# A two-layer gated-DeltaNet backbone on one core: one masked product stored at once, context units placed in another phase, masks of four heads in one instruction

## The chip, the core and the metric

The kernel runs on one NeuronCore of a Trainium2 chip. The metric is the device time of one execution in microseconds (us). One engine multiplies matrices (PE), one works on vectors (DVE), one evaluates functions (ACT), one is general (POOL); nearly all transfers are started from the queue of SP. The engines run side by side and wait for each other through semaphores. All of PE's instructions stand in an order that the program writes out itself; the order on the other engines is made by a scheduler from priorities.

## What is computed

```
for layer in 2 layers:                     # 2048 latent tokens, 256 context tokens, width 1024
    h = rms_norm(x) * (1 + scale) + shift
    xa, bg, cg, za, q, k, v, zb, b, a = split(h @ w_in)       # 4096 columns and 16
    q, k, v = silu(conv3(q, k, v)); q, k normalised           # 4 heads of 128
    o = deltanet(q, k, v, b, a, forwards) + deltanet(..., backwards)
    y = concat(bg * conv3(cg * xa) * silu(za), rms_norm(o) * silu(zb))
    x += gate * (y @ w_out)                # context tokens: in the first layer alone
out = rms_norm(x)
```

The latent scans of a direction start from the state that the context scan of that direction ended in. All products are float32 quality: a projection is three products of split operands.

## The kernel before

**Chunks and tasks.** The 18 groups of 128 tokens are five chunks: 0 is the context (2 groups), 1 to 4 are the latents (4 groups each). `project` (L326) is one task: 24 products that give 128 columns of the projection for one chunk. Columns come in units: 12 of q, k and v (`qkv`, three for each head), 16 of the convolution mixer (`mix`), 4 of the gate `zb`. `phase` (L584) runs a list of tasks; each unit's weights are loaded, split by ACT (L312) and subtracted by POOL (L314), or half by DVE and half by POOL where `shared` is set, which is so when the phase has one chunk alone. `edge` (L1066) runs units over one chunk and then backwards over the next; `pairs` runs each unit over all chunks before the next unit. A layer is: a short context phase, phase 1 (chunks 1 and 2), phase 2 (chunks 3 and 4), and `output` (L958), with 48 products for each token group.

**The written order.** Between the products of a task `pump` (L177) lets other jobs issue PE work. A job is a generator that yields how many us of PE work, by the planner's clock `Order.now`, are to pass before it goes on, or a condition. `until` (L188) moves that clock on when a condition is not met yet: then the jobs' work stands in the order with no projection between it.

**Preparation (`delta`, L619).** A job J handles 16 items (a head and a group): two heads over 8 groups. J00 and J01 belong to phase 1 of the first layer, J02 and J03 to its phase 2, J10 to J13 to the second layer; J0c and J1c are the context's. Each item loads its record (L637) into one of three buffers and two rows (L639), transposes and multiplies on PE (L658, L660), masks two products by `dm` in one DVE instruction into U (L669) and stores k and v (L675); `ITEM` = 3.8 us are yielded between items. At item 8 a job waits until the job before it is done (L648), because three U tiles of 8 KB are all there are. Then comes the tail: coefficients (L679 to L697), the inversion of 32x32 blocks by 31 steps of two DVE instructions (L728, L730), transfers that reorder blocks (L710 to L735), a yield of 50 + 2n us (82 for 16 items, L751), the merging products on PE (from L754 on; the first of them is called z1 here), and the store of U to the record in DRAM (L804).

**Scans (`scan`, L808).** A scan goes over groups: it loads a record tile `rc` of 1.5 MB (one of two buffers), masks two parts of it for each head on POOL (L832), and runs five products for each of four heads. The scans take turns with the token loads by a lock named "rc". F0a and F0b are the forward latent scans of the first layer (8 groups each), F0c the backward one (16), C00 and C01 the context's; F1a to F1c are those of the second layer. F0b waits for F0a and J03. A group's output waits for F0c's result of it.

**Order around the change.** In the first layer the 20 context tasks of `mix` and `zb` stand in phase 2 (L1122). They read context activations that are loaded again (`reload`, L384) into two of the U buffers, so that job ("again", L1117) waits for J03. In the second layer no such tasks exist. J jobs start when unit `qkv[5]` or `qkv[11]` is done and the gates of both chunks are there (L1079 to L1083, L1101, L1111).

Of the kernel before, what the change touches and what calls it, by code (L numbers as in the profile page):

```python
# [32 lines left out]
RECB = 3  # L33
HOP = 2.2
# [3 lines left out]
ITEM = 3.8  # L38
# [3 lines left out]
class Pool:  # L42
# [5 lines left out]
    def tile(self, shape, dtype, tag=None, bufs=None, name=None):  # L48
# [9 lines left out]
        assert size == own, (tag, size, own)  # L58
# [4 lines left out]
def hybrid_backbone_kernel(ctx_stack: ExitStack, tc: tile.TileContext,  # L63
# [369 lines left out]
    def chunks_in(L, ps, loaded=()):  # L433
# [5 lines left out]
        z = {}  # L439
        for n, (p, i) in enumerate(halves):  # L440
# [10 lines left out]
            if i + 2 == m:  # L451
                done.add(("h", L.l, p))
                if p in (0, 1, 3):
                    z = {"z": small_tile("g_z" if p else "g_z0"), "g": g0, "n": 0}
                yield from logits(L, p, z["z"][:, z["n"]:z["n"] + m, :])
                z["n"] += m
                if p in (0, 2, 4):
                    spawn(("g", L.l, p), gates(L, z["g"], z["n"], z["z"][:, 0:z["n"], :]))
# [72 lines left out]
    def qkv_unit(L, s, h):  # L531
# [4 lines left out]
        def consume(ci, a):  # L536
# [6 lines left out]
            nc.sync.dma_start(out=L.rec_d[g0:g0 + n, :, h, 128 * (3 - s):128 * (4 - s)].rearrange("g p t -> p g t"), in_=y.rearrange("p (g t) -> p g t", t=128))  # L543
# [40 lines left out]
    def phase(L, units, tasks, after={}, ready={}):  # L584

        w = dict(ready)
        seen = []
        left = {}
        for j, p in tasks:
# [29 lines left out]
    def delta(L, items, with_out, before):  # L619
# [26 lines left out]
        yield 7.0  # L646
        for i, (h, g) in enumerate(items):
            if i == 8 and before is not None:  # L648
                yield lambda: before in done
            if i % 8 == 0:  # L650
                U.append(dp.tile([128, 8, 2, 128], F32, tag="u", bufs=3, name="U"))
# [3 lines left out]
            with urgent():  # L655
                tp = pt()
                for s in range(s0, 3):
# [11 lines left out]
                nc.vector.tensor_tensor(U[i // 8][:, i % 8, 0:w_, :], kp[:, 0:128 * w_].rearrange("p (s t) -> p s t", t=128),  # L669
                                        dm.unsqueeze(1).to_broadcast([128, w_, 128]), ALU.mult)  # L670
# [524 lines left out]
```

## Time and profile before

| | us |
|---|---|
| median of 3 runs (3021.18 to 3025.34) | 3023.2 |
| the profiled execution | 3020.82 |
| its span, first to last instruction | 3019.1 |
| PE busy in it | 2652.3 (88%) |
| mean granted clock of PE | 0.947 of full speed |

The page gives each engine's busy time, the waits say whom an engine waited for, the chain says what ended last at each moment, and the windows give the busy time of each engine in a stretch. A busy PE is not PE at its peak: records of products overlap, so PE's rate is read from start to start.

### The profile page before, as it was taken

The numbers are of one execution on the slowest core, as the hardware profiler recorded it, in microseconds if no ns is written. First come the engines' busy times: TensorE is split into PE (matmuls) and PEld (weight loads), VectorE is DVE, ScalarE is ACT, GpSimd is POOL, SyncE is SP. The second block draws the span as 40 slices with busy tenths as digits, with TensorE's granted clock in tenths as the row PEclk, the third lists the DMA queues.
The fourth block names the chain that finished last, engine by engine and source line by source line (L and its number), as shares of the span: only waits on it lengthen the run. The fifth ranks groups of instructions, "written<-read, shape, count | busy, mean of one in ns | idle before, by whom it ended". The sixth has DMA issues, their size and how long they took to land. (4 is left out here: it accounts for less than half of the span.)

```text
span 3019.1 us, 48183 instructions
## 1 busy us (share of the span) xinstructions
PE 2652.3 (88%) x17431; PEld 2214.9 (73%) x17431; DVE 1652.2 (55%) x3972; ACT 1165.4 (39%) x3072; POOL 1012.4 (34%) x1045
## 2 busy tenths in 40 slices
PE   5898899899999489769998899998999999677898
PEld 3776778668878379768777677776788777566787
DVE  3676655555573444544133676655556746345665
ACT  2535433433544322443013544333535432423442
POOL 1332333322233113454344423332322323114543
PEclk9899999999999789889999899999999999889999
DMA  6545734356554365675755556434566533566754
GB/s 205 162 132 168 223 91 139 104 191 193 172 145 120 82 202 187 237 259 189 235 160 162 166 135 187 129 101 100 180 191 179 147 113 90 182 244 204 251 179 117
DMA packets 573323, 502.18 MB, mean 166 GB/s; under 512 B 100010, under 2 KB 528540, under 8 KB 564380
## 3 DMA queue, kind: packets, MB, share of 16 engines
q1 hardware_dynamic: 573084, 499.10, 55.1%
q8 instruction: 138, 2.26, 0.3%
q14 instruction: 101, 0.83, 0.1%
HBM read 369.86 MB, written 129.14 MB: 165 GB/s over the span
## 5 line engine op out<-in xcount | busy, mean ns | idle before, releaser
L153 PE MATMUL d<-h,whi 128*128 128x512 f32 x2048 | 861.3, 421 | 20.6 <-ACT whi L312 15.5
L153 PE MATMUL d<-h,wlo 128*128 128x512 f32 x2048 | 815.7, 398 | 41.2 <-POOL wlo L314 41.2
L153 PE MATMUL d<-l,whi 128*128 128x512 f32 x2048 | 809.8, 395 | 0.0
L314 POOL TENSOR_TENSOR wlo<-raw,whi 128x1024 fp32r<-128x1024 f32 (+1 forms) x178 | 417.0, 2343 | 564.0 <-ACT whi L312 539.8
L153 PEld LDWEIGHTS d<-h,wlo 128*128 128x128 f32 x2048 | 392.1, 191 | 135.1 <-POOL wlo L314 49.2
L153 PEld LDWEIGHTS d<-h,whi 128*128 128x128 f32 x2048 | 393.4, 192 | 104.0 <-ACT whi L312 18.3
L153 PEld LDWEIGHTS d<-l,whi 128*128 128x128 f32 x2048 | 393.6, 192 | 73.5
L153 PE MATMUL d<-who,yy 128*128 128x512 f32 x1088 | 362.8, 401 | 19.4 <-ACT yy L991 18.8
L312 ACT CAST whi<-raw 128x1024 fp32r<-128x1024 f32 x178 | 186.3, 1047 | 192.4 <-PE d L153 127.2
L153 PEld LDWEIGHTS d<-who,yy 128*128 128x128 f32 x1088 | 206.0, 189 | 66.8 <-ACT yy L991 19.0
L832 POOL TENSOR_SCALAR_AFFINE_SELECT rc<-rc 128x256 f32<-128x256 f32 (+1 forms) x288 | 111.0, 422 | 307.8 <-DMA rc<-rec_d 266.6
L153 PE MATMUL d<-wlo,yy 128*128 128x512 f32 x544 | 213.4, 392 | 0.0
L668 POOL TENSOR_TENSOR nk<-nk,phalf 128x1 f32<-128x1 f32 x144 | 85.6, 594 | 362.6 <-DVE nk L667 328.9
L728 DVE TENSOR_TENSOR tmp<-Lt,X 64x31 f32<-64x31 f32 (+15 forms) x310 | 134.8, 435 | 60.7 <-DMA Lt<-blk 48.8
L730 DVE TENSOR_TENSOR X<-X,tmp 64x31 f32<-64x31 f32 (+15 forms) x310 | 127.8, 412 | 7.2
L992 POOL TENSOR_TENSOR yy<-ys,yy 128x512 fp32r<-128x512 f32 x68 | 94.1, 1395 | 102.5 <-ACT yy L991 96.2
L340 DVE SCALAR_TENSOR_TENSOR y<-d,par,y 128x504 f32<-128x504 f32 (+2 forms) x116 | 80.0, 689 | 87.3 <-ACT y L337 87.0
L153 PE MATMUL d<-hc,whi 128*128 128x256 f32 x320 | 100.7, 315 | 28.6 <-ACT whi L312 23.8
L541 ACT ACTIVATE d<-y 128x512 f32<-128x512 f32 (+1 forms) x116 | 65.5, 565 | 143.4 <-DVE y L341 129.1
L153 PEld LDWEIGHTS d<-wlo,yy 128*128 128x128 f32 x544 | 103.2, 190 | 18.6
L884 DVE SCALAR_TENSOR_TENSOR r<-c,eg,rc 128x128 f32<-128x128 f32 x272 | 76.7, 343 | 69.4 <-PE c L153 68.6
L896 DVE TENSOR_SCALAR wk<-c,cs 128x128 f32<-128x128 f32 x288 | 80.8, 342 | 61.8 <-PE c L153 61.6
(397 smaller groups left out, 4605.2 us busy)
## 6 DMA issues: line engine op xcount, KB each, us to landing
rc<-rec_d SPq DMA_DIRECT2D x68, 1536.0 KB, 7.1
raw<-in_w_in_dram SPq DMA_DIRECT2D x178, 512.0 KB, 4.8
rec<-rec_d SPq DMA_DIRECT2D x136, 192.0 KB, 2.5
wm<-in_w_mod_dram SPq DMA_DIRECT2D x24, 1024.0 KB, 8.2
rec_d<-y SPq DMA_DIRECT2D x96, 256.0 KB, 3.0
rows<-row_d SPq DMA_DIRECT2D x144, 128.0 KB, 3.7
rec_d<-rec SPq DMA_DIRECT2D x144, 128.0 KB, 2.5
ys<-y_d SPq DMA_DIRECT2D x68, 256.0 KB, 3.8
```

The source lines that it names most:

```text
L153: nc.tensor.matmul(o, a, b, start=start, stop=stop)
L312: nc.scalar.copy(hi, raw)
L314: eng.tensor_sub(lo[:, k], raw[:, k], hi[:, k].bitcast(F32))
L340: nc.vector.scalar_tensor_tensor(d3[:, :, 1:segs], s3[:, :, 0:segs - 1], w[0], d3[:, :, 1:segs], ALU.mult, ALU.add)
L541: nc.scalar.activation(a, y, AF.Tanh, scale=0.5)
L668: nc.gpsimd.tensor_tensor(nk[:, i:i + 1], nk[:, i:i + 1], phalf[:, 0:1], ALU.pow)
L728: nc.vector.tensor_tensor(t3, L3[:, j + 1:32, j:j + 1].to_broadcast([2 * nb, m_, k]), X3[:, j:j + 1, 0:k].to_broadcast([2 * nb, m_, k]), A ...
L730: nc.vector.tensor_sub(X3[:, j + 1:32, 0:k], X3[:, j + 1:32, 0:k], t3)
L832: nc.gpsimd.affine_select(out=m, in_=m, pattern=[[0, w_], [1 - 2 * d, 128]], compare_op=ALU.is_ge, fill=0.0, base=0, channel_multiplier=2 ...
L884: nc.vector.scalar_tensor_tensor(r[:, h, :], at(p1, h), e_(L.eg, h), vn[h], ALU.mult, ALU.subtract)
L896: nc.vector.tensor_scalar(wk[:, h, :], at(p2, h), cs(2 + d, h), None, ALU.mult)
L992: nc.gpsimd.tensor_sub(l_, yr, h_.bitcast(F32))
```

## The change

The record of an item is laid out anew (k, v, second product P, kT, qT, first product V). P, the masked second product, goes from the item straight into the record and is stored with k and v; U holds V alone, at half the size, in the same ring of 24 KB. A job's wait for the job before moves from item 8 to the end of the items. An item's load becomes two DMAs. `ITEM` is 2.8; J jobs start at `qkv[0]` and `qkv[8]` and wait for their second chunk's gates and second head inside. Gates are computed for each chunk (five times a layer, before three). For J02, J03, J12 and J13 (`fast`) the tail has high priority and yields 60. The 20 context tasks stand in phase 1, on activations loaded again into the two `rc` buffers, under the "rc" lock, after C01; the tokens of chunks 3 and 4 are loaded once they are done. Weights are halved between DVE and POOL for every unit that is not followed by another task of its own. A scan masks all heads in one instruction (V first, then P) and yields 0.7 ahead of its fifth product.

```diff
-ITEM = 3.8
+ITEM = 2.8
...
-            h = L.hs[0] = h_tiles(0)
+            h = L.hs[0] = [dp.tile([128, 3, D], F32R, tag="rc", bufs=2, name=t).rearrange("p a b -> p (a b)")[:, 0:256 * KT].rearrange("p (k t) -> p k t", t=256)
+                           for t in ("hc", "lc")]
...
+                z = small_tile("g_z")[:, 0:m, :]
+                yield from logits(L, p, z)
+                spawn(("g", L.l, p), gates(L, g0, m, z))
...
+        single = {j: tasks[t + 1:t + 2] == [] or tasks[t + 1][0] != j for t, (j, p) in list(enumerate(tasks))[::-1]}
-                w[j] = weights(w_in[L.l], units[j][0], len(set(p for _, p in tasks)) == 1)
+                w[j] = weights(w_in[L.l], units[j][0], single[j])
...
-                nc.sync.dma_start(out=rec[:, 1:4 - s0].rearrange("p s t -> p (s t)"), in_=L.rec_d[g, :, h, 128:512 - 128 * s0])
+                nc.sync.dma_start(out=rec[:, 1, :], in_=L.rec_d[g, :, h, 128:256])
+                nc.sync.dma_start(out=rec[:, 2:4 - s0].rearrange("p s t -> p (s t)"), in_=L.rec_d[g, :, h, 384:640 - 128 * s0])
...
-        yield 7.0
+        yield 9.0
         for i, (h, g) in enumerate(items):
-            if i == 8 and before is not None:
-                yield lambda: before in done
             if i % 8 == 0:
-                U.append(dp.tile([128, 8, 2, 128], F32, tag="u", bufs=3, name="U"))
+                U.append(dp.tile([128, 8, 128], F32, tag="u", bufs=3, name="U"))
+            if i + 2 in wants:
+                yield lambda: done.issuperset(wants[i + 2])
...
-                nc.vector.tensor_tensor(U[i // 8][:, i % 8, 0:w_, :], kp[:, 0:128 * w_].rearrange("p (s t) -> p s t", t=128),
-                                        dm.unsqueeze(1).to_broadcast([128, w_, 128]), ALU.mult)
+                nc.vector.tensor_mul(U[i // 8][:, i % 8, :], kp[:, 0:128], dm)
...
-                nc.sync.dma_start(out=L.rec_d[g, :, h, 0:256], in_=rec[:, 0:2].rearrange("p s t -> p (s t)"))
+                if with_out:
+                    nc.vector.tensor_mul(rec[:, 2, :], kp[:, 128:256], dm)
+                nc.sync.dma_start(out=L.rec_d[g, :, h, 0:256 + 128 * (w_ - 1)], in_=rec[:, 0:1 + w_].rearrange("p s t -> p (s t)"))
             yield ITEM
         held.discard("items")
+        if before is not None:
+            yield lambda: before in done
+        first = tc.high_priority(offset=HP) if fast else nullcontext()
+        first.__enter__()
...
-        yield 50.0 + 2.0 * n
+        first.__exit__(None, None, None)
+        yield 60.0 if fast else 50.0 + 2.0 * n
...
-                for h in hd:
-                    m = rc[:, h, 4:4 + w_, :]
-                    nc.gpsimd.affine_select(out=m, in_=m, pattern=[[0, w_], [1 - 2 * d, 128]], compare_op=ALU.is_ge, fill=0.0, base=0, channel_multiplier=2 * d - 1)
+                for z in (5, 2) if with_out else (5,):
+                    m = rc[:, :, z, :]
+                    nc.gpsimd.affine_select(out=m, in_=m, pattern=[[0, NH], [1 - 2 * d, 128]], compare_op=ALU.is_ge, fill=0.0, base=0, channel_multiplier=2 * d - 1)
...
+            yield 0.7 if with_out else HOP
+            with urgent():
                 if with_out:
                     pw = pscan("c1")
...
-            yield HOP - (0.9 if with_out else 0.0)
+            yield 0.6 if with_out else 0.0
...
-        jobs = {("unit", qkv[5]): J(0), ("unit", qkv[11]): J(1), ("unit", mix[3][1]): load_second}
+        jobs = {("unit", qkv[0]): J(0), ("unit", qkv[5]): flag("qkv", l, 0, 1), ("unit", qkv[8]): J(1), ("unit", qkv[11]): flag("qkv", l, 0, 3)}
+        tasks = edge(qkv[:5], 1, 2) + pairs(qkv[5:] + mix[0], (1, 2))
+        if L.ctx_out:
...
+            behind((f"C{l}1",), "again", again, "rc")()
+            behind((f"J{l}1",), "mods", lambda: mod_job(l, L.P, 8, 12))()
+            tasks += pairs(sum(mix[1:], []), (1, 2, 0)) + pairs(mix[0] + zb, (0,))
+            jobs["chunk", 0] = lambda: (done.add(("ctx", l)), load_second())
...
-            behind((f"J{l}3",), "again", again)()
-            tasks += pairs(zb, (3, 4)) + pairs(mix[2] + mix[3], (3, 4, 0)) + pairs(zb + mix[0] + mix[1], (0,))
-        else:
-            tasks += pairs(mix[2] + mix[3], (3, 4)) + edge(zb, 3, 4)
-        phase(L, units, tasks, jobs)
+        phase(L, units, edge(qkv[:5], 3, 4) + pairs(qkv[5:] + sum(mix, []), (3, 4)) + edge(zb, 3, 4), jobs)
```

## Rows read from the trace of the kernel before

**Rows 1.** The page's first part: busy time, share of the span and instructions of each engine.

```profile
PE 2652.3 (88%) x17431; PEld 2214.9 (73%) x17431; DVE 1652.2 (55%) x3972; ACT 1165.4 (39%) x3072; POOL 1012.4 (34%) x1045
```

**Rows 2.** The windows view, cut where the program's stages change: phase 1 of the first layer; phase 2 up to its first context task; the gap there; the last stretch of context tasks; the first output stage; phase 2 of the second layer; its output stage up to the end of F1c, in two pieces. Columns: stretch and length, busy us (and instructions) of PE, its weight loads, DVE, ACT, POOL, then the granted clock, the DMA share and GB/s.

```profile
130.00:623.20 493.20, 449.02 (x3025) 364.32 (x3023) 310.22 (x721) 212.74 (x553) 159.55 (x152) 0.97 0.50 140
623.20:1005.70 382.50, 364.25 (x2313) 301.44 (x2314) 211.80 (x535) 167.07 (x449) 117.36 (x122) 0.98 0.56 166
1005.70:1098.90 93.20, 37.40 (x569) 32.85 (x568) 41.95 (x106) 15.01 (x28) 8.11 (x15) 0.65 0.46 133
...
1243.90:1356.00 112.10, 70.27 (x554) 68.22 (x552) 51.38 (x124) 48.89 (x146) 57.81 (x58) 0.84 0.77 254
1356.00:1616.00 260.00, 252.75 (x1373) 203.21 (x1373) 81.68 (x206) 48.88 (x140) 107.81 (x96) 0.99 0.61 185
...
2152.00:2613.00 461.00, 439.83 (x2889) 365.68 (x2889) 259.22 (x626) 191.03 (x481) 144.73 (x138) 0.97 0.53 153
2613.00:2742.00 129.00, 79.27 (x599) 71.55 (x598) 60.68 (x170) 37.21 (x118) 25.31 (x55) 0.81 0.65 227
2742.00:2912.00 170.00, 151.49 (x913) 131.96 (x914) 106.80 (x262) 74.69 (x273) 84.41 (x102) 0.96 0.69 228
```

**Rows 3.** The waits of PE over the whole span: engine, tile and line that waited, for whom; us in total, times, longest us.

```profile
PE d L153 <- POOL wlo L314: 42.8, 17, 6.4
...
PE t L153 <- DMA tf<-blk: 37.3, 1, 37.3
```

**Rows 4.** The same view for 2613 to 2742 us alone.

```profile
PE c L153 <- DMA rc<-rec_d: 21.9, 4, 17.6
```

**Rows 5.** The timeline of J03's tail (start us, length us, engine, line, operation): the first coefficient on DVE and the first merging product z1 on PE with the wait ahead of it.

```profile
993.72 0.16 DVE L679 TENSOR_SCALAR rk<-ssk 128x16 f32<-128x16 f32 x1
...
1048.60 0.32 PE L153 MATMUL t<-tf,U 32*32 32x32 f32 x4 [37.27 <-DMA tf<-blk]
```

**Rows 6.** The chain of work that ended last, in order of time (start us, length us, what, how many): products of a scan, the first coefficient of J13, its z1, its last store, and the outputs at the end.

```profile
2235.33 1.79 PE c L153 x16
...
2501.68 1.12 DVE rk L679
...
2602.95 1.86 PE t L153 x128
...
2631.23 8.02 DMA rec_d<-U
...
2917.00 88.46 PE d L153 x390
```

**Rows 7.** The windows view of line 669 alone, one instruction for each item: J12's 16 items, and the first 8 of J13. Columns: stretch and length, DVE busy us (and items), clock, DMA share, GB/s.

```profile
2268.00:2352.00 84.00, 6.64 (x16) 1.00 0.61 180
2360.00:2405.00 45.00, 3.32 (x8) 1.00 0.59 144
```

**Rows 8.** The windows view of line 730 alone; the bounds are the first L728 and the end of the last L730 of the inversions of J03, J12 and J13.

```profile
1018.40:1041.80 23.40, 10.63 (x31) 0.50 0.00 0
2373.60:2409.40 35.80, 12.55 (x31) 1.00 0.49 138
2523.40:2556.50 33.10, 12.39 (x29) 1.00 0.18 48
```

**Rows 9.** The windows view of line 896 alone, four instructions for each scan tile: the context's scans C00 and C01, the last five tiles of F0c, F1a, and F1c.

```profile
300.00:362.00 62.00, 4.45 (x16) 0.94 0.79 234
...
1335.00:1415.00 80.00, 5.62 (x20) 0.87 0.63 208
2200.00:2291.00 91.00, 8.98 (x32) 0.96 0.68 212
...
2711.00:2912.00 201.00, 17.99 (x64) 0.93 0.66 219
```

**Rows 10.** POOL's groups by shape (busy us and mean ns behind the bar): the masks of a scan for one head, two products and one.

```profile
L832 POOL TENSOR_SCALAR_AFFINE_SELECT rc<-rc 128x256 f32<-128x256 f32 x272 | 106.7, 429 | 290.2 <-DMA rc<-rec_d 256.3 <-PE c L153 11.6 <-PE d L153 9.0
...
L832 POOL TENSOR_SCALAR_AFFINE_SELECT rc<-rc 128x128 f32<-128x128 f32 x16 | 4.2, 302 | 17.6 <-DMA rc<-rec_d 10.3 <-PE c L153 7.3
```

**Rows 11.** The timeline inside J12's inversion: POOL subtracts weights, and one inversion step on DVE.

```profile
2382.97 2.43 POOL L314 TENSOR_TENSOR wlo<-raw,whi 128x1024 fp32r<-128x1024 f32 x1 [2.11 <-ACT whi L312]
...
2383.17 2.47 DVE L730 TENSOR_TENSOR X<-X,tmp 128x220 f32<-128x220 f32 x1
```

**Rows 12.** The waits of SP's queue over the whole span, and below it those of 2300 to 2350 us: the item loads.

```profile
SPq L637 <- DMA rec_d<-rec: 287.0, 121, 7.5
...
SPq L637 <- DMA rec_d<-rec: 21.7, 10, 3.8
```

**Rows 13.** The waits of PE from 130 to 623 us: two that belong to items.

```profile
PE t L160 <- DMA rec<-rec_d: 6.1, 2, 4.0
...
PE t L160 <- ACT rec L674: 3.5, 2, 3.1
```

**Rows 14.** The timeline of two products of a context task, one after the other.

```profile
1639.75 0.28 PE L153 MATMUL d<-lc,whi 128*128 128x256 f32 x1
1639.87 0.28 PE L153 MATMUL d<-hc,wlo 128*128 128x256 f32 x1
```

**Rows 15.** The windows view of a stretch in which items, an inversion and the convolutions of q, k and v meet (columns as in rows 2), and the masked product of an item by its durations (line 669, ns min/median/max; the shape 128x128 is that of the second layer's context).

```profile
850.00:900.00 50.00, 46.34 (x209) 37.77 (x209) 41.66 (x111) 20.59 (x71) 14.54 (x14) 0.97 0.52 138
...
L669 DVE TENSOR_TENSOR U<-o,dm x111: 269/415/425, 140.9 to 2502.7; 128x256 f32<-128x256 f32 x103, 128x128 f32<-128x128 f32 x8
```

More of the change, by code (lines that the diff above doesn't have):

```diff
@@ L33 @@
 RECB = 3
+REC = (512, 384, 128)
 HOP = 2.2
@@ L57, in tile @@
         ring, own = self.rings[tag]
-        assert size == own, (tag, size, own)
+        assert size == own or tag == "u", (tag, size, own)
         return ring.tile(shape, dtype, name=name)
@@ L438, in chunks_in @@
             xs.append(tokens_in(L, *halves[len(xs)]))
-        z = {}
         for n, (p, i) in enumerate(halves):
@@ L617, in phase, with delta @@
             pump()
-    def delta(L, items, with_out, before):
+    def delta(L, items, with_out, before, wants={}, fast=False):
         n = len(items)
@@ L871, in scan @@
                 yield t + RECORD - Order.now
-            kn, vn, kT, qT, V_, P_ = ([rc[:, h, s, :] for h in hd] for s in range(6))
+            kn, vn, P_, kT, qT, V_ = ([rc[:, h, s, :] for h in hd] for s in range(6))
             cs = lambda k, h: L.cs[:, g, k, h:h + 1]
@@ L1081, in J @@
             items = [(h, g) for h in hs for g in gs]
-            return behind((("g", l, 4 if i > 1 else 2),) + wants, f"J{l}{i}",
-                          lambda: delta(L, items, True, f"J{l}{i - 1}" if i else f"J{l}c"))
+            p = 3 if i > 1 else 1
+            return behind((("g", l, p),) + wants, f"J{l}{i}",
+                          lambda: delta(L, items, True, f"J{l}{i - 1}" if i else f"J{l}c", wants={4: (("g", l, p + 1),), 8: (("qkv", l, i // 2, hs[1]),)}, fast=i > 1))
         until(("h", l, 0))
@@ L1097, in layer, with again @@
         free = {("chunk", 1): flag("free", l, 3), ("chunk", 2): flag("free", l, 4)}
-        more = {}
-        if l == 0:
-            more[qkv[11]] = behind(("J01",), "mods", lambda: mod_job(l, L.P, 8, 12))
-        jobs = {("unit", qkv[5]): J(0), ("unit", qkv[11]): J(1), ("unit", mix[3][1]): load_second}
-        if l == 0:
-            jobs["unit", mix[0][0]] = more[qkv[11]]
-        phase(L, units, edge(qkv[:5], 1, 2) + pairs(qkv[5:] + sum(mix, []), (1, 2)) + edge(zb, 1, 2), {**jobs, **free})
+        jobs = {("unit", qkv[0]): J(0), ("unit", qkv[5]): flag("qkv", l, 0, 1), ("unit", qkv[8]): J(1), ("unit", qkv[11]): flag("qkv", l, 0, 3)}
+        tasks = edge(qkv[:5], 1, 2) + pairs(qkv[5:] + mix[0], (1, 2))
+        if L.ctx_out:
+            done.discard(("h", l, 0))
+            def again():
+                reload(L)
+                done.add(("h", l, 0))
+                yield lambda: ("ctx", l) in done
+            behind((f"C{l}1",), "again", again, "rc")()
+            behind((f"J{l}1",), "mods", lambda: mod_job(l, L.P, 8, 12))()
+            tasks += pairs(sum(mix[1:], []), (1, 2, 0)) + pairs(mix[0] + zb, (0,))
+            jobs["chunk", 0] = lambda: (done.add(("ctx", l)), load_second())
+        else:
+            tasks += pairs(sum(mix[1:], []), (1, 2))
+            jobs["unit", mix[3][1]] = load_second
+        phase(L, units, tasks + edge(zb, 1, 2), {**jobs, **free})
         lat = list(range(2, NG))
@@ L1110, in layer @@
         wo = {}
-        jobs = {("unit", qkv[5]): J(2, *(("mods",) if l == 0 else ())), ("unit", qkv[11]): J(3),
+        jobs = {("unit", qkv[0]): J(2, *(("mods",) if l == 0 else ())), ("unit", qkv[5]): flag("qkv", l, 1, 1),
+                ("unit", qkv[8]): J(3), ("unit", qkv[11]): flag("qkv", l, 1, 3),
                 ("chunk", 3): lambda: out_weights(L, 0, wo), ("chunk", 4): lambda: out_weights(L, 4, wo)}
-        tasks = edge(qkv[:5], 3, 4) + pairs(qkv[5:] + mix[0] + mix[1], (3, 4))
-        if L.ctx_out:
-            done.discard(("h", l, 0))
-            def again():
-                reload(L)
-                done.add(("h", l, 0))
-                yield 0.0
-            behind((f"J{l}3",), "again", again)()
-            tasks += pairs(zb, (3, 4)) + pairs(mix[2] + mix[3], (3, 4, 0)) + pairs(zb + mix[0] + mix[1], (0,))
-        else:
-            tasks += pairs(mix[2] + mix[3], (3, 4)) + edge(zb, 3, 4)
-        phase(L, units, tasks, jobs)
+        phase(L, units, edge(qkv[:5], 3, 4) + pairs(qkv[5:] + sum(mix, []), (3, 4)) + edge(zb, 3, 4), jobs)
         at_tile = {}
```

37 lines of the change are left out of this document (15 added, 22 removed).

## The prediction

> **What bounds the kernel now.** I read the page's engine line first: PE is busy 88% of the span [rows 1], so PE's work is the floor and its idle time the stock that a change of order can take from. The windows by stage say where that stock lies: length less PE busy is 44 us in phase 1 of the first layer, 18 us in the start of its phase 2, 56 us in the gap, 42 us in the last context stretch, 7 us in its outputs; in the second layer 21 us in phase 2, then 50 and 19 us in the outputs [rows 2]. The clock falls with the idle time: 0.65 of full speed in the gap, 0.84 in the context stretch, 0.81 after phase 2 of the second layer, 0.97 or more where PE runs on [rows 2]; products there run partly at 1.2 instead of 2.4 GHz. Then the waits: one single wait of 37.3 us for the reordered inverse of J03 [rows 3, 5], and 21.9 us for scan records behind J13 [rows 4]. Both say the same: at the end of each phase 2 the preparation J03 or J13 is late, and nothing else stands in PE's order. In the first layer the projections that could fill the gap read context activations that wait for J03's buffers; in the second no projections are left.
>
> **Prices on PE.** A latent product starts every 88.46 / 390 = 0.227 us [rows 6], so a task is 24 x 0.227 = 5.45 us and an output group 48 x 0.227 = 10.9 us. A scan product starts every 1.79 / 16 = 0.112 us [rows 6]; five products, four heads, two instructions each give 40 x 0.112 = 4.5 us for a scan tile. A context product takes 0.12 us [rows 14], a context task 24 x 0.12 = 2.9 us.
>
> **When J12 and J13 end after the change.** J12 starts at the tenth task instead of the twelfth: 2 x 5.45 us, and about 1.6 scan tiles of 4.5 us between them (F1a runs there, a tile in 91 / 8 = 11.4 us [rows 9]), 18 us; the first yield is 2 longer, so its items start 16 us earlier than some 2270 [rows 7], about 2254. Items come every 84 / 16 = 5 us or a little less now [rows 7], which is ITEM, the item's own PE work and the step of the planner; with ITEM 1.0 less I take 4.0 us, 64 us for 16: to 2318. J13's items no longer wait at the eighth for J12: 2318 + 10 + 64 = 2392. The tail asks for z1 63 us after the first coefficient (60 and a step of the planner). What the other engines need is 54.9 us in J03, where POOL was idle (993.72 to 1048.60 [rows 5]); in J13 the inversion was 33.1 instead of 23.4 us [rows 8], which gives 65 us. So z1 comes about on time, 2318 + 63 = 2381. From z1 to the last store J13 took 2631.2 - 2603.0 = 28 us [rows 6]: J12 is done at 2409, after J13's items. J13's tail then runs 2409 + 63 + 28 + 2 = 2502, against 2631: **129 us earlier**.
>
> **Second layer.** F1b starts at 2502 instead of 2640 and takes 8 x 11.4 = 91 us plus the 11 us that the planner holds a record: done at 2604, inside phase 2. Phase 2 ended at 2152 + 461 + 5 = 2618 [rows 2]; F1b's PE work adds 8 x 4.5 = 36 us, and some 5 tiles of F1c that fit ahead of its end another 22: 2676. The outputs then need 16 x 10.9 = 174 us, the 11 tiles left of F1c 50 us, other PE work 14 us (of the 277 us from 2742 to the end, 166 are outputs that are left, 58 are 13 tiles of F1c, 18.5 idle and 7 low clock [rows 2], 14 the drain after the last product [rows 6]), the drain 14 us, and half the idle time, 9 us: 2676 + 261 = 2937. **Gain 82 us.** F1c is not the bound: at 201 / 16 = 12.6 us a tile [rows 9] it ends near 2810, and outputs would last to 2937 anyway.
>
> **First layer.** Phase 1 takes 12 context tasks in threes at 2.9 us and 8 alone, where weights for each task must be made: 12 tasks of that kind took 112 us with scans between them [rows 2]; I take 3.9 us with the halved subtraction, bounds 2.9 and 9.3. Sum 35 + 31 = 66 us: phase 1 ends at 623 + 66 = 689. Phase 2 becomes the second layer's: 382 us for the first 50 tasks [rows 2], 14 x 5.45 = 76, F0b 36, J03's merging products some 10 (128 took 1.86 us [rows 6], with waits between): 504. By the second layer's distances F0b ends 2604 - 2152 = 452 us after the phase begins, and 4 tiles of F0c fit behind it, 18 us: 689 + 522 = 1211. The outputs took 260 us [rows 2] with F0c's last 5 tiles [rows 9]; 12 instead of 5 add 32: 1503, against 1616. **Gain 113 us**: the gap, the context stretch and their clock.
>
> **Costs.** The two halves of a masked product cost DVE 2 x 0.27 instead of 0.415 us [rows 15], 0.13 us on each of 136 items, 17 us of DVE beside PE; four more calls of gates are some 4 us of DVE each (an estimate: 24 small operations of 0.16 us as in [rows 5]). Where DVE is fullest it has 41.7 of 50 us [rows 15]; three more items in 50 us at 1.2 us and the split's 1.5 us make 47: no bound yet, but PE waits grow. I charge 0.15 us to each of 128 latent items, 19 us, bounds 0 and 0.4 (phase 1 has 9.6 us of such waits in its 40 items, 0.24 each [rows 13]). For the four fast tails z1 may come before its data: bounds 0 and 12 us each, taken 5, 20 us with the clock; 12 because J12's inversion took 35.8 us. The new `zb` edge in the first layer has waits like those for `wlo` [rows 3], 10 us taken, bounds 0 and 15. An item's further DMA is one more issue on SP; the scan's new yield only moves 0.7 of 1.3 us: nothing, hidden by the 11 us hold; bounds -5 and 5. Masks: 302 ns for 128 and 429 for 256 columns [rows 10] make 683 for 512, so two instead of four take 1.37 instead of 1.72 us, V for all heads after 0.68; POOL is idle for its record when it starts [rows 10], so at most 0.35 us for each of 32 backward tiles, 0 to 11 us, taken 0. The reload waits for C01 and can hold PE at the 35th task if it is late; C01 was over at 362 [rows 9], and 34 tasks of 493 / 64 = 7.7 us [rows 2] put that task at 130 + 262 = 392, so 0, bounds 0 and 30.
>
> Sum: 82 + 113 - 19 - 20 - 10 = 146, and against that the earlier edges with halved weights, 0 to 10, taken 5: **151 us**. 3020.8 - 151 = 2870 for the profiled execution (its span and 1.7 us around it); the median is 2.4 us above it: **2872**.
>
> **A rule against a term.** In J12 one inversion step, 0.34 us on average with POOL idle (10.63 / 31 [rows 8]), took 2.47 us while POOL subtracted weights for 2.43 us [rows 11]; with POOL idle the 31 steps took 23.4 us, beside it 35.8 [rows 8]. The Trainium skill, page "SBUF — State Buffer", section "Who interferes with whom", says that a DVE instruction with two SBUF inputs and a GpSimd instruction that reads SBUF exclude each other for a whole instruction; the trace agrees. By that rule high priority cannot shorten the tail to its free length, and the halved weight subtraction saves less than half.
>
> **Rivals.** (1) *POOL holds the inversion.* As told ahead of the rule, as a mechanism here: each fast tail meets five or six weight subtractions and, where a scan runs, longer masks; inversions of 36 to 40 us make the tail 68 to 72 us, 5 to 9 beyond what the order allows, and each stall starts a stretch at 1.2 GHz, some 4 us. Four tails: 36 to 52 us instead of 20, so 2888 to 2904. For it: two of three inversions are that long [rows 8]. Against: at a yield of 82 z1 waited once alone, where nothing else stood in the order [rows 3].
> (2) *DVE is the bound where items crowd.* If 47 of 50 us is too full and PE waits for convolutions, each of the eight latent jobs' 64 us grows by a fifth: 8 x 13 = 104 us less gain, 2976. For it: 41.7 of 50 us already [rows 15]; against: those stretches have PE 92% busy.
> (3) *The jobs do not overlap after all*, as the ring hands out U in order and other tiles use it. Then J13's items 8 to 15 still follow J12's end: 2409 + 42 + 63 + 30 = 2544, 42 us later, of which F1b inside the phase hides about half: 20 us in each layer, 2912.
> (4) *Slower: SP's queue starves the items.* SP waits 2.4 us before an item load for the store of an item before (287 / 121), 21.7 of 50 us in a quiet stretch [rows 12], and all weight loads queue behind it. At 4.0 us an item, with more stored per item and two loads, these waits may no longer fit. It decides at 151 / 128 = 1.2 us of PE stall per latent item; at 1.6 us the kernel takes 3023 + 128 x 0.4 = 3074. Against: PE lost only 6.1 us to record loads in all of phase 1 [rows 13].
>
> **How the numbers follow.** Forecast with its bounds (gain 110 to 220) 0.58; rival 1 0.12; rival 3 0.08; rival 2 0.11; a gain under 0.2%, the ends of 2 and 4 meeting, 0.02; rival 4 0.05; beyond the forecast's best (all 367 us of idle time more than halved) 0.04. Range 2805 to 2960 holds the forecast, rivals 1 and 3 and the near side of 2. A measurement of this kernel tells 0.2% from no change: faster 0.93, same 0.02, slower 0.05.
>
> **What would show it.** Right: no wait of 37 us for `tf`; F0b and F1b's tiles inside phase 2, with PE over 95% busy there; context tasks between 400 and 690; items 4 us apart; J13's last store near 2400 on the new axis (2502 less the first layer's gain); outputs without waits for `rc`. Wrong: waits of z1 above 10 us (rival 1), waits for L542 or L341 (2), a pause at the eighth item (3), waits of transposes for `rec` and of tasks for `whi` behind L637 (4).

## The result, and the profile after

| | before | after |
|---|---|---|
| median, us (runs) | 3023.61 (4: 3021.18 to 3025.34) | 2926.74 (4: 2920.88 to 2935.34) |
| profiled execution, us | 3020.82 | 2922.38 |
| its span, us | 3019.1 | 2920.7 |
| mean granted clock | 0.947 | 0.960 |

The ratio is 0.9682, 95% interval 0.9654 to 0.9711: 97 us faster. 151 us were forecast. The time lies in the range, in its upper half.

The page's engine line (columns as in [rows 1]):

```profile
PE 2652.7 (91%) x17459; PEld 2209.5 (76%) x17459; DVE 1689.4 (58%) x4273; ACT 1162.1 (40%) x3090; POOL 942.7 (32%) x895
```

PE's busy time is that of [rows 1] to 0.4 us: no work was saved on PE, and the 98 us of span are idle time, 366.8 before and 268.0 after. DVE has 37 us more: the split masked product, the halved subtractions, and four more calls of the gates.

The windows by stage (columns as in [rows 2]): phase 1, phase 2 and outputs of the first layer; phase 1, phase 2, and the outputs up to the end of F1c in the second.

```profile
139.10:710.00 570.90, 524.58 (x3656) 434.05 (x3655) 329.86 (x819) 231.70 (x588) 167.08 (x157) 0.96 0.50 143
710.00:1256.00 546.00, 507.87 (x3445) 426.70 (x3445) 324.61 (x861) 222.00 (x599) 156.17 (x153) 0.97 0.60 179
1256.00:1554.60 298.60, 290.71 (x1715) 240.23 (x1713) 131.38 (x347) 87.53 (x291) 137.85 (x126) 0.99 0.74 234
...
1607.70:2108.40 500.70, 457.01 (x3080) 370.28 (x3078) 308.65 (x805) 211.18 (x521) 147.51 (x143) 0.95 0.49 135
2108.40:2655.80 547.40, 508.40 (x3448) 426.37 (x3447) 327.41 (x863) 221.74 (x603) 154.37 (x151) 0.97 0.57 173
2655.80:2825.00 169.20, 156.84 (x946) 136.29 (x946) 118.73 (x274) 82.57 (x285) 88.57 (x83) 0.99 0.77 254
```

The gap, the context stretch and the hole ahead of F1c of [rows 2] are gone: none of the stretches shown runs below a clock of 0.95, where three of before ran at 0.65, 0.84 and 0.81. The same stages in a row, against before and against the forecast, lengths in us:

| stage | before | forecast | after |
|---|---|---|---|
| start, up to phase 1 | 130 | 130 | 139 |
| first layer, phase 1 | 493 | 559 | 571 |
| phase 2 | 733 | 522 | 546 |
| outputs | 260 | 292 | 299 |
| second layer, its start | 52 | 52 | 53 |
| phase 1 | 484 | 484 | 501 |
| phase 2 | 590 (to the first output) | 524 | 547 |
| rest | 277 | 261 | 265 |

The forecast's column adds to 2824, and it charged 44 us of costs net (19 + 20 + 10 - 5) on top. After has 2921: the costs came to 97 us, and the table places them: 9 in the start, 12 and 17 in the two phases 1, 24 and 23 in the two phases 2, 7 in the outputs, 5 in the other two rows. The forecast's charges can be placed too: some 5 us in each of the four phases for the items, 10 more in each phase 2 for the tails, 10 in the first phase 1 for the edge. By that the first phase 1 came at its price or under it; what is missing is 12 us in phase 1 of the second layer, 9 in each phase 2, 9 in the start and 7 in the outputs.

PE's waits over the whole span; below them, the largest from 2656 to 2825 us, the stretch that answers to [rows 4]:

```profile
PE t L161 <- DMA rec<-rec_d: 36.5, 18, 4.0
PE c L161 <- ACT hf L426: 27.0, 8, 7.8
PE d L154 <- ACT whi L313: 23.2, 10, 9.9
...
PE t L161 <- ACT rec L672: 15.4, 8, 4.0
PE d L154 <- DVE wlo L315: 13.5, 10, 2.1
...
PE t L154 <- DMA tf<-blk: 7.1, 3, 3.1
PE d L154 <- POOL wlo L315: 2.4, 2, 1.9
...
PE c L154 <- DVE wk L901: 2.6, 2, 2.0
```

The one wait of 37.3 us for `tf` [rows 3] is three of 7.1 us together; the 21.9 us for `rc` [rows 4] have no successor. New at the top are waits for the loads of item records (36.5 us in 18) and for the prepared tokens `hf` (27.0 in 8). In the kernel before, these were

```profile
PE c L160 <- ACT hf L424: 14.5, 5, 8.0
...
PE t L160 <- DMA rec<-rec_d: 6.9, 3, 4.0
```

So the two holes became many waits, most of them of 1 to 4 us.

Line 668 alone (669 before [rows 7]), one instruction an item: J02, J03, J12, J13.

```profile
811.00:891.00 80.00, 4.61 (x16) 0.96 0.65 200
907.00:990.00 83.00, 4.53 (x16) 0.92 0.56 151
2211.00:2291.00 80.00, 4.61 (x16) 0.98 0.65 200
2307.00:2389.00 82.00, 4.53 (x16) 0.92 0.57 151
```

Sixteen items take 80 to 83 us, 5.0 to 5.2 each: not 4.0. From the first to the last of these instructions it is 79 us for J12, where it was 77 before. J13's have no pause at the eighth any more.

The timeline of J12's tail and of J13's end (columns as in [rows 5]):

```profile
2289.94 0.17 DVE L683 TENSOR_SCALAR rk<-ssk 128x16 f32<-128x16 f32 x1
...
2363.09 0.25 PE L154 MATMUL t<-tf,U 32*32 32x32 f32 x4 [2.37 <-DMA tf<-blk]
...
2502.05 0.38 SPq L809 DMA_DIRECT2D rec_d<-U  x1
```

The tail takes 73 us from the first coefficient to z1, with a wait of 2.4 us. J13's last store is issued 2502 - 2108 = 394 us after its phase begins; 350 were forecast, and before the store lay 479 us after it.

### The profile page after: what moved, and what is told of

Read it like the earlier page. It is cut to its first block, busy times and chain, and to the rows that moved or that the text cites. A ratio compares the mean times of both kernels' runs of the same rounds, so it can differ in the third digit from the quotient of the medians.

```text
span 2920.7 us, 48653 instructions
## 1 busy us (share of the span) xinstructions
PE 2652.7 (91%) x17459; PEld 2209.5 (76%) x17459; DVE 1689.4 (58%) x4273; ACT 1162.1 (40%) x3090; POOL 942.7 (32%) x895
## 4 chain that ended last, share of the span: by engine, by line
PE 53%; DMA 18%; DVE 14%; issue 5%; ACT 5%; POOL 3%; SPq 2%; POOLq 0%; ACTq 0%; DVEq 0%
PE d L154 41%; PE c L154 5%; PE t L154 3%; DMA rec_d<-rec 3%; DMA rc<-rec_d 2%; DMA raw<-in_w_in_dram 2%; DVE tmp L732 2%; PE o L154 2%; DMA rec<-rec_d 1%; DVE X L734 1%; DVE y L341 1%; PE t L161 1%; DVE y L342 1%; POOL wlo L315 1%; DVE wlo L315 1%
## 5 line engine op out<-in xcount | busy, mean ns | idle before, releaser
L154 PE MATMUL d<-h,whi 128*128 128x512 f32 x2048 | 878.1, 429 | 17.1 <-ACT whi L313 12.9
L315 POOL TENSOR_TENSOR wlo<-raw,whi 128x1024 fp32r<-128x1024 f32 (+1 forms) x176 | 368.0, 2092 | 674.8 <-ACT whi L313 655.4
L154 PE MATMUL d<-who,yy 128*128 128x512 f32 x1088 | 373.0, 403 | 0.4 <-POOL yy L999 0.4
L837 POOL TENSOR_SCALAR_AFFINE_SELECT rc<-rc 128x512 f32<-128x512 f32 x140 | 93.1, 688 | 245.9 <-DMA rc<-rec_d 206.9
L732 DVE TENSOR_TENSOR tmp<-Lt,X 64x31 f32<-64x31 f32 (+15 forms) x310 | 144.0, 464 | 40.2 <-DMA Lt<-blk 34.3
L161 PE MATMUL t<-ident,rec 128*128 128x128 f32 x424 | 74.5, 285 | 69.4 <-DMA rec<-rec_d 36.5
L161 PEld LDWEIGHTS t<-ident,rec 128*128 128x128 f32 x424 | 54.3, 145 | 97.8 <-issue 32.2
L734 DVE TENSOR_TENSOR X<-X,tmp 64x31 f32<-64x31 f32 (+15 forms) x310 | 120.2, 388 | 6.5
L905 ACT ACTIVATE w<-c,cs 128x128 f32<-128x128 f32 x272 | 78.0, 371 | 105.0 <-DVE wk L901 103.3
```

The source lines that it names most:

```text
L154: nc.tensor.matmul(o, a, b, start=start, stop=stop)
L161: nc.tensor.transpose(o, a, ident[0:a.shape[0], 0:a.shape[0]])
L315: eng.tensor_sub(lo[:, k], raw[:, k], hi[:, k].bitcast(F32))
L732: nc.vector.tensor_tensor(t3, L3[:, j + 1:32, j:j + 1].to_broadcast([2 * nb, m_, k]), X3[:, j:j + 1, 0:k].to_broadcast([2 * nb, m_, k]), A ...
L734: nc.vector.tensor_sub(X3[:, j + 1:32, 0:k], X3[:, j + 1:32, 0:k], t3)
L837: nc.gpsimd.affine_select(out=m, in_=m, pattern=[[0, NH], [1 - 2 * d, 128]], compare_op=ALU.is_ge, fill=0.0, base=0, channel_multiplier=2 ...
```

## Experiments

Times are set against the kernel before on the same chip as a ratio with its interval; the time given is the median. Not all kernels ran on the same chip, so a difference between two of them is that of their ratios times 3024 us; by the intervals of the ratios, such a difference is uncertain by some 8 to 13 us (an estimate). Each kernel ran four times, e8 ten times and e12 five times. The change itself has 0.9682 [0.9654, 0.9711]. My theory at the start (A): both mechanisms work as forecast, and the 54 us that are missing are paid at the items, whose record buffers and order do not bear the closer pace. Rivals named in the expectations: waits that only change their name, and costs in other places.

**e3, the first layer's part alone.** The kernel before, with the context tasks, the reload and the token loads of the change in phase 1.

```diff
-        jobs = {("unit", qkv[5]): J(0), ("unit", qkv[11]): J(1), ("unit", mix[3][1]): load_second}
...
+            behind((f"C{l}1",), "again", again, "rc")()
+            more[qkv[11]]()
+            tasks += pairs(sum(mix[1:], []), (1, 2, 0)) + pairs(mix[0] + zb, (0,))
...
+        phase(L, units, edge(qkv[:5], 3, 4) + pairs(qkv[5:] + sum(mix, []), (3, 4)) + edge(zb, 3, 4), jobs)
```

> The kernel before with one part of the change: the 20 context tasks of the first layer in phase 1, reloaded into the rc buffers. Theory A (J03 and J13 are late at the end of phase 2, and moving tasks only takes away what filled that wait): the wait for tf leaves the gap and appears as waits for rc records after the first layer's phase 2, as in the second layer; gain 15 to 40 us, 2983 to 3008, and the second layer unchanged. Rival (the move itself is what pays): gain of 70 us and more, below 2953.

2988.09, ratio 0.9885 [0.9856, 0.9913]: 35 us faster. Phase 1 grows to 564 us, phase 2 shrinks to 474, but the outputs take 415 instead of 260. The windows view and PE's waits (whole span) show why:

```profile
1170.00:1290.00 120.00, 77.06 (x579) 66.65 (x578) 57.05 (x154) 31.92 (x98) 27.29 (x53) 0.88 0.73 252
...
PE c L153 <- DMA rc<-rec_d: 36.8, 10, 18.3
```

The gap is gone and J03 is still late (its last store comes 500 us after phase 2 begins, 454 in the kernel before), so the wait for it moved behind phase 2, into F0b's and F0c's records: 43 us of 120 idle, just as the second layer has it in [rows 2]. Moving the tasks alone gives a third of the gain.

**e4, all of the change but that part.** The context tasks back in phase 2, loaded again in the ring of U behind J03.

```diff
+        tasks = edge(qkv[:5], 3, 4) + pairs(qkv[5:] + mix[0] + mix[1], (3, 4))
...
+            behind((f"J{l}3",), "again", again)()
+            tasks += pairs(zb, (3, 4)) + pairs(mix[2] + mix[3], (3, 4, 0)) + pairs(zb + mix[0] + mix[1], (0,))
```

> The changed kernel with the context tasks back in phase 2 behind J03, reloaded into the U ring. Theory A: the second layer keeps its 38 us of gain; in the first layer J03 is done some 100 us earlier, so the tasks that read the reloaded activations wait less; 2940 to 2975. Rival (the move itself pays, overlapping jobs alone do not): 2990 to 3020, with a wait of 30 us or more for tf left in the first layer.

2972.67, ratio 0.9832 [0.981, 0.9854]: 51 us faster. 35 + 51 = 86 of the change's 97, so the two parts nearly add up.

**e1, four record buffers instead of three.** Paid for in SBUF by single `eg` and `atot` and a smaller `g_z`.

```diff
-RECB = 3
+RECB = 4
```

> The changed kernel with four record buffers for the items instead of three (paid for with single eg and atot tables and a half-size z tile). Theory A, the items of 4 us are held back by the turnaround of three record buffers (store lands, then load lands, and PE waits 36.5 us for rec): PE's waits for rec loads fall below 12 us and the time falls by 20 to 40 us, to 2885 to 2905. Theory B, DVE is too full where items crowd: the waits move to other tiles and the time stays within 8 us of 2927. Theory C, the queue of SP (issues in order) is what holds the loads: waits fall by half at most, 5 to 15 us gained.

2912.74, ratio 0.9635 [0.9608, 0.9661]: 14 us better than the change, the intervals overlapping slightly. PE's waits for records and coefficients over its whole span:

```profile
PE t L161 <- ACT rec L672: 22.1, 14, 5.0
...
PE t L154 <- DMA tf<-blk: 15.9, 3, 5.9
...
PE t L161 <- DMA rec<-rec_d: 8.3, 4, 3.2
```

The load's wait fell from 36.5 to 8.3 us, as A wanted; half of that came back as waits of the same transposes for ACT's writes of `rec` and as waits for `tf`. A sized the gain too high; it is of the size of C, but C had the waits fall by half at most.

**e2, the old pace of the items.**

```diff
-ITEM = 2.8
+ITEM = 3.8
```

> The changed kernel with ITEM back at 3.8. Theory A (buffers limit the items, which come 4.5 to 5.3 us apart though 4.0 was planned): slower planning removes PE's waits for rec (36.5 us to about 10) and costs little at the end of the phases, as the items came no faster anyway: 2905 to 2930. Rival: the denser items are what brings J03 and J13 forward; then F0b and F1b start some 25 us later each and the time rises to 2945 to 2965.

2944.89, ratio 0.9734 [0.9712, 0.9756]: 16 us slower than the change. J12's 16 items take 84 us and J13's 104 instead of 80 and 82, and the phases 1 are no shorter (568, 502). So the closer pace pays, and it isn't what the phases 1 suffer from: A falls there. The 1.0 us less in the planner is 0.25 (J12) and 1.4 us (J13) less between items.

**e5, no overlap in the phases 1.** J00, J01, J10, J11 start and wait as before; J02, J03, J12, J13 overlap.

```diff
+            if i == 8 and before is not None and not fast:
+                yield lambda: before in done
...
-        jobs = {("unit", qkv[0]): J(0), ("unit", qkv[5]): flag("qkv", l, 0, 1), ("unit", qkv[8]): J(1), ("unit", qkv[11]): flag("qkv", l, 0, 3)}
+        jobs = {("unit", qkv[5]): J(0), ("unit", qkv[11]): J(1)}
```

> The changed kernel with the overlap of jobs undone in phase 1 alone: J00, J01, J10 and J11 start at qkv[5] and qkv[11] and wait at item 8 for the job before, as before the change; J02, J03, J12 and J13 as in the change. Theory A (overlap in phase 1 brings nothing, as no scan waits for J01 or J11 early, and crowds the items into the stretch where the convolutions run): phase 1 falls by 8 to 15 us in each layer, 2897 to 2912. Rival (what made phase 1 longer, 17 us in the second layer, are the halved weights, the gates of each chunk or the dearer items themselves): 2922 to 2932.

2908.1, ratio 0.9612 [0.9578, 0.9645]: 21 us (0.7%) better than the change. The two phases 1:

```profile
139.30:699.60 560.30, 518.25 (x3657) 428.82 (x3655) 342.76 (x819) 230.79 (x588) 167.50 (x157) 0.97 0.51 146
...
1595.40:2084.10 488.70, 453.92 (x3072) 367.04 (x3071) 314.17 (x803) 209.76 (x520) 149.59 (x143) 0.96 0.50 138
```

Both are shorter, by 11 and 12 us. Nothing waits for J01 or J11 there, so having them early buys nothing and crowds the phase. In the profile 12 us come back behind the last phase 2, which takes 277 us to the end instead of 265; why is open.

**e9, no overlap anywhere.** The early starts, ITEM 2.8 and the fast tails stay; every job waits at its eighth item for the job before.

```diff
+            if i == 8 and before is not None:
+                yield lambda: before in done
```

> The changed kernel with the wait at item 8 put back for every job (the early starts, the 2.8 us and the high priority stay). Theory A (in phase 2 the overlap is what lets F0b and F1b run inside the phase; in phase 1 it only crowds): phase 1 is 8 to 12 us shorter in each layer as with the overlap undone there alone, and J03 and J13 end some 30 to 40 us later, which costs 15 to 25 us at the end of each phase 2: 2920 to 2945, thus 15 to 35 above the run with the overlap in phase 2 alone (2908). Rival (the overlap pays nothing anywhere, the early starts and the quick items do it all): 2900 to 2912.

2925.44, ratio 0.9671 [0.9656, 0.9685]: level with the change, 18 us behind e5. Its phases 1 are e5's (563, 489), so it is the overlap and not the early start that costs there; and in the phases 2 the overlap is worth about what it costs in the phases 1. The two profiles are 15 us apart: 6 in phase 2 and rest of the second layer (829 against 824), none to speak of in phase 2 and outputs of the first (847 against 846), 3 in the first phase 1, and the rest in the starts of the layers, where the two kernels have the same code. The gain of the overlap in phase 2 is therefore 6 to 18 us, not settled closer. J13's last eight items stand alone here, behind J12's merging products, and come some 4.2 us apart with three record buffers while PE is busy throughout (line 670, the same product):

```profile
2379.00:2412.00 33.00, 2.27 (x8) 1.00 0.43 131
```

**e6, no fast tails**: 82 us and the usual priority.

```diff
-                          lambda: delta(L, items, True, f"J{l}{i - 1}" if i else f"J{l}c", wants={4: (("g", l, p + 1),), 8: (("qkv", l, i // 2, hs[1]),)}, fast=i > 1))
+                          lambda: delta(L, items, True, f"J{l}{i - 1}" if i else f"J{l}c", wants={4: (("g", l, p + 1),), 8: (("qkv", l, i // 2, hs[1]),)}, fast=False))
```

> The changed kernel with the tails of J02, J03, J12 and J13 at normal priority and a yield of 82 us instead of 60. Theory A: each tail is 20 us longer, J03 and J13 end some 40 us later, F0b and F1b start later and end behind phase 2: 2945 to 2965. Rival 1 of the prediction (POOL holds the inversion, so z1 cannot come earlier and 60 only stalls PE): within 10 us of 2927, with fewer waits of z1 for tf and tb.

2931.9, ratio 0.9682 [0.9651, 0.9713]: no difference that these runs resolve. J13's last store comes 28 us later (422 instead of 394 after the phase begins) and z1 never waits over 2.1 us. The same 30 us around J12's merging products, in the change and then here (columns as in [rows 2]):

```profile
2360.00:2390.00 30.00, 19.27 (x386) 14.96 (x385) 15.62 (x47) 13.78 (x40) 5.05 (x8) 0.77 0.35 82
```

```profile
2360.00:2390.00 30.00, 28.75 (x460) 23.24 (x459) 21.50 (x61) 15.94 (x39) 13.59 (x15) 1.00 0.40 100
```

In the change PE is idle 10.7 us there and its clock falls to 0.77; it waits for J12's `tf` (2.4), `tb` (2.6) and `v` (4.6). Here it is idle 1.3 us, and J13's 16 items take 75 us instead of 82. So the fast tails cost PE some 10 us in each layer, and the earlier stores are worth about the same, as far as these runs resolve it.

**e7, weights halved only where phases have one chunk.**

```diff
-                w[j] = weights(w_in[L.l], units[j][0], single[j])
+                w[j] = weights(w_in[L.l], units[j][0], len(set(p for _, p in tasks)) == 1)
```

> The changed kernel with weights halved between DVE and POOL only in phases of one chunk, as before the change; the 8 context tasks that stand alone then have their weights made by POOL. Theory (halving saves 0.7 us a weight in the edges, and DVE pays for it): PE's waits for wlo come back, 10 to 20 us, and the time rises by 5 to 20 us, 2932 to 2947. Rival (the halves keep DVE from the convolutions and lengthen phase 1): the time falls by 5 to 15 us, 2912 to 2922.

2938.35, ratio 0.9698 [0.9673, 0.9724]: 5 us slower by the ratio, which the intervals do not resolve. In PE's waits of this kernel POOL's weights are back:

```profile
PE d L154 <- POOL wlo L315: 26.2, 16, 3.7
```

**e8, the masks alone.** The kernel before, with one instruction for all heads.

```diff
-                for h in hd:
-                    m = rc[:, h, 4:4 + w_, :]
...
+                for z in range(4, 4 + w_):
+                    m = rc[:, :, z, :]
```

> The kernel before with one part of the change: the masks of a scan record in two instructions of four heads instead of four of one head. Theory: POOL saves 0.35 us on each of 64 record tiles and is not on the path of most of them; within 6 us of 3024, unless the longer holds of POOL delay DVE, 0 to 10 us slower. Rival (masks are on the path of every scan tile that waits for its record): 8 to 15 us faster, most of it in the outputs of the second layer.

3028.71, ratio 1.0005 [0.999, 1.002]: nothing, as the forecast took it.

**e10, e5 with four record buffers.**

```diff
-RECB = 3
+RECB = 4
...
+            if i == 8 and before is not None and not fast:
```

> The overlap undone in phase 1 alone together with four record buffers. If both losses are separate (crowding of phase 1, 19 us; waits for rec, 14 us), they add: 2890 to 2900. If both treat the same loss: 2903 to 2910.

2900.67, ratio 0.9589 [0.9572, 0.9605]: 7 us better than e5, intervals overlapping, though the waits for record loads fell from 25.9 to 2.4 us.

**e11, e5 with the gates for two chunks at once**, three calls a layer as before; the jobs start behind the gates of both chunks.

```diff
-                spawn(("g", L.l, p), gates(L, g0, m, z))
+                if p in (0, 1, 3):
+                    z = {"z": small_tile("g_z" if p else "g_z0"), "g": g0, "n": 0}
...
+                if p in (0, 2, 4):
+                    spawn(("g", L.l, p), gates(L, z["g"], z["n"], z["z"][:, 0:z["n"], :]))
...
-            p = 3 if i > 1 else 1
+            p = 4 if i > 1 else 2
```

> The overlap undone in phase 1 alone, and the gates computed as before the change, for two chunks at once, with the jobs' start behind them. Theory (the two further calls of gates a layer take DVE and ACT ahead of the first tasks, and phase 1 begins 9 us later than before the change): 4 to 14 us less than the 2908 without this edit, with the first latent task near 131 instead of 139. Rival (gates are hidden, and the jobs of phase 2 start later without the split): 2908 to 2920.

2880.69, ratio 0.9524 [0.9508, 0.954]: 27 us better than e5, more than I had expected. The windows view of the gates' tile `sm` alone over the span, the change and then e11 (DVE's instructions come ahead of ACT's):

```profile
0.00:2920.00 2920.00, 53.95 (x210) 4.50 (x20) 0.96 0.58 172
```

```profile
0.00:2870.00 2870.00, 33.15 (x126) 2.89 (x12) 0.97 0.59 175
```

By all lines of the gates it is 69.6 us in 280 instructions against 43.1 in 168 (44.5 in the kernel before): a call costs DVE 28 instructions and some 7 us whether for one chunk or two, 26 us for the four calls. PE's waits in e11:

```profile
PE d L154 <- ACT whi L313: 30.4, 12, 10.0
PE t L161 <- DMA rec<-rec_d: 30.1, 16, 4.3
...
PE c L161 <- ACT hf L426: 11.1, 4, 7.4
```

The wait for `hf`, 29.6 us in 8 in e5, is 11.1 in 4. Phase 1 begins at 129 us instead of 139, as in the kernel before.

**e12, all three**: e11 with four record buffers.

```diff
-RECB = 3
+RECB = 4
...
+                if p in (0, 2, 4):
+                    spawn(("g", L.l, p), gates(L, z["g"], z["n"], z["z"][:, 0:z["n"], :]))
...
+            if i == 8 and before is not None and not fast:
+                yield lambda: before in done
```

> The overlap undone in phase 1 alone, the gates as before the change, and four record buffers (eg and atot tables single, one z tile). If the three losses are separate, four buffers take another 5 to 12 us from 2881: 2868 to 2876, a ratio near 0.950 to the kernel before, and PE's waits for rec loads (30 us with three buffers) fall below 10 us. If the waits for rec only hide others: 2877 to 2884.

2864.14, ratio 0.946 [0.9437, 0.9483]: the fastest, 5.4% below the kernel before and 2.3% below the change; the granted clock is 0.969. It is 19 us better than e11, more than expected. The four stages that matter, phase 1 and phase 2 of each layer:

```profile
131.30:678.20 546.90, 514.47 (x3650) 428.75 (x3648) 346.20 (x817) 230.42 (x585) 170.08 (x158) 0.97 0.53 150
1567.30:2046.70 479.40, 448.39 (x3066) 362.62 (x3065) 311.38 (x775) 209.03 (x515) 148.92 (x143) 0.97 0.51 140
678.20:1217.90 539.70, 507.10 (x3449) 427.25 (x3449) 323.94 (x844) 222.60 (x602) 155.88 (x153) 0.97 0.61 183
2046.70:2587.90 541.20, 508.62 (x3457) 428.27 (x3456) 321.63 (x841) 223.97 (x601) 156.10 (x151) 0.97 0.59 177
```

## Why the prediction was right in kind and 54 us short

**What held.** J03 and J13 were what bounded the ends of both phases 2. With them earlier, PE's hole behind the phase closed in each layer, and e3 shows that it doesn't close without it. Phase 1 of the first layer takes the context tasks at the forecast's price: 66 us were forecast, 71 more it is in e3 and 78 in the change, 11 of those being the overlap (e5). F0b and F1b lie inside their phases 2, and PE is busy all through both (88.0 and 89.0 us): line 901, the scans' (896 in [rows 9]), gives F0b, F1b and F1c as

```profile
1112.00:1200.00 88.00, 9.01 (x32) 1.00 0.69 233
2511.00:2600.00 89.00, 9.01 (x32) 1.00 0.66 222
2612.00:2815.00 203.00, 18.06 (x64) 0.97 0.74 246
```

with F1b done 492 us after its phase begins, 452 forecast, and F1c 707 us after it, 658 forecast (its 2810 was on the axis of the kernel before, whose phase began at 2152). Masks at 512 columns take 688 ns, 683 forecast, and e8 shows them to be worth nothing; halved weights are worth 5 (e7, not resolved), 5 taken.

**The step that failed is the paragraph on costs**, 44 us where 97 were paid. Three of its terms or silences had a share:
- *The gates.* "Four more calls of gates are some 4 us of DVE each" stood "beside PE". They are some 7 us each, 28 instructions of 0.25 us instead of 24 of 0.16, and they don't lie beside PE's work: taken back they give 27 us (e11 against e5), where the whole of their DVE time is 26. Starts of the program show it without any other part of the change: 129 to 132 us in the kernels with three calls a layer (before, e3, e8, e11, e12), 136 to 143 in the nine with five.
- *The overlap in the phases 1.* The forecast placed the gain of overlapping jobs in phase 2 and did not price the same edit where nothing waits for it. Phase 1 of the second layer, which has no context tasks, took 491 to 507 us in the six kernels with the overlap and the split gates (the change, e1, e2, e4, e6, e7), 485 to 489 in e5, e9 and e10 without the overlap, 479 to 481 in e11 and e12 without either, and 484 to 486 in the kernel before, e3 and e8. The price is 21 us in all (e5).
- *The pace of the items.* "With ITEM 1.0 less I take 4.0 us" gave 64 us for 16; it was 80 to 83. J13's items end 280 us after its phase begins, where 240 were forecast, and 257 for the end of J12 that its tail would wait for; from there the tail took 79 instead of 63 us and the rest up to the last store 34 instead of 30, which makes 394 instead of 350. The third record buffer has a share in it that one more buffer shows: 14 us (e1), 7 (e10) and 19 (e12), the middle one unresolved. It isn't all that sets the pace: in e12 the loads' waits are gone, and line 674, the same product there, gives 72 us for J12's 16 items but 89 for J13's:

```profile
2146.00:2218.00 72.00, 4.57 (x16) 0.95 0.68 207
2234.00:2323.00 89.00, 4.46 (x16) 0.88 0.55 144
```

The planned 4.0 us are nearly reached where items meet nothing (4.2 in e9). In the change, J13's first 12 items take 55 us and its last 4, among J12's merging products, 27 (line 668):

```profile
2307.00:2362.00 55.00, 3.39 (x12) 1.00 0.70 188
2362.00:2389.00 27.00, 1.14 (x4) 0.75 0.30 76
```

27 + 21 + 7 = 55 us, against 54 missing; with 19 for the buffer, as in e12, it is 67. That 55 meets 54 is partly luck. Each of the figures is uncertain by some 8 to 13 us, and they do not fit stage by stage: in e12, which has all three remedies, the phases 1 lie some 27 and 9 us below the forecast with its charges, the phases 2 some 3 and 2 above it, and what is left behind the last phase 2 lies 13 above (274 against 261).

**The tails.** Fast tails were charged 20 us, and that was not too much: PE is idle 10.7 us around J12's merging products (e6) and 9.6 around J02's, and the clock is lower in both places. e6 gives the net alone, in which the earlier stores about make up for this. The bound on z1 held (7.1 us of waits for `tf` and 7.2 for `tb`, in three tails each). The tails took 73 to 80 us, more than the 63 forecast and the 68 to 72 of rival 1. For J12's the reason is on record, as its z1 waits for data; J13's z1 waits for nothing, so there it is the written order that comes late. The item's own extra product, 0.13 us of DVE forecast, is 2 x 0.28 us instead of 0.415, 0.15.

**The rivals.** Rival 1 shows in half of the tails: J12's inversion takes 40.1 us and its z1 waits, J13's takes 33.3 and its z1 doesn't (line 734; of the two long inversions of [rows 8] only one, 35.8 us, came near the 36 to 40 that the rival took):

```profile
2316.40:2356.50 40.10, 12.59 (x31) 1.00 0.60 175
2411.50:2444.80 33.30, 12.83 (x31) 1.00 0.22 62
```

Rival 2 doesn't show: where J12's and J13's items run, the waits for the convolutions are not among the first, and the record loads are (10.1 us of 178). Rival 3 didn't come, since the pause at the eighth item is gone, and e9 made it: worth 6 to 18 us instead of the 40 forecast. Rival 4's sign is the opposite: SP's waits ahead of item loads fell from 287 us [rows 12] to

```profile
SPq L635 <- DMA rec_d<-rec: 208.1, 111, 5.6
```

though those loads are what PE waits for most. With four buffers most of PE's wait goes (8.3 us in e1) while SP's is nearly the same (202.1 us), so it was the buffers' turn and not the queue.

**What stays open.** Why the gates' 26 us of DVE cost 27 on the path: that their chain stands ahead of the tokens' preparation on DVE and ACT fits the waits for `hf`, but those fell by 18.5 us only, and e11 also moved the jobs' starts. And what keeps J12's items 5 us apart: another record buffer takes some 5 of their 79 us (74 in e1), and what they meet besides (scans of the same phase, weights, convolutions) was not taken apart. The 7 us that the outputs take over the forecast are not explained.

## What to carry to other kernels

An edit that helps where something waits for it is priced again in every other place where the same code runs: the overlap of jobs paid in phase 2 and cost as much in phase 1, so that overlapping everywhere was level with nowhere (e9), and overlapping in phase 2 alone was some 20 us better than either. A chain of small instructions costs by its count, not by its data, so calling it for smaller pieces "to be earlier" has to be charged at full length and on the path until a trace shows the cover. When two large holes close, read the many small waits that are left as one sum: here three cheap remedies together took 67 us off the change (e12).

## What the runs showed of the hardware

A DVE instruction with one tensor input and a scalar for each partition was held up by POOL as the inversion's two-input steps were [rows 11]. The timeline of the change inside J12's items:

```profile
2267.72 2.39 POOL L315 TENSOR_TENSOR wlo<-raw,whi 128x1024 fp32r<-128x1024 f32 x1 [3.65 <-ACT whi L313]
...
2268.05 2.14 DVE L661 TENSOR_SCALAR dm<-rows,cum 128x128 f32<-128x128 f32 x1
```

The same instruction has a median of 0.28 us over its 144 runs; here it ends with POOL's. The Trainium skill, page "SBUF — State Buffer", section "Who interferes with whom", counts `tensor_scalar` among the operations that can take the port pair that DVE shares with GpSimd, in its two-port modes; this row agrees with that, and which mode the instruction ran in no row shows. Three of the 144 took over 1 us, and each of them overlapped a subtraction on POOL. So not only two-input steps can be held up by it; what that costs the kernel no run isolates.
